# A two-layer decoder trunk in fp32: the depthwise convolution divided anew between TensorE and VectorE, and weights kept split for the second half

## The chip, the cores and the metric

The kernel runs on one core of one Trainium2 chip, in one launch. Its time is that of the device, in microseconds (us), from one execution to the next; the median of several runs is given. The engines named below are TensorE (PE: matrix products, with its weight loads PEld), VectorE (DVE), ScalarE (ACT), GpSimd (POOL) and SyncE (SP, which here issues the DMAs).

## The reference

The input x is 2048 rows of 1024 float32 numbers. Two layers with residuals follow, and a last RMSNorm. Layer 0 projects, pools over four windows, runs a state space scan, gates and projects back. Layer 1 is the one the change touches:

```
def _odd_mixer(h, w_in, conv_w, conv_b, ln_g, ln_b, w_out):
    proj = jnp.einsum('bsd,de->bse', h, w_in)
    val, gt, z = ...
    g = (val * jax.nn.sigmoid(gt)).astype(jnp.float32)
    c = lax.conv_general_dilated(
        g, kern, window_strides=(1,), padding=[(CONV_KERNEL - 1, 0)],
        dimension_numbers=('NWC', 'WIO', 'NWC'), feature_group_count=CONV_CHANNELS)
    c = c + conv_b.astype(jnp.float32)
    mu = jnp.mean(c, axis=-1, keepdims=True)
    cc = c - mu
    var = jnp.mean(cc * cc, axis=-1, keepdims=True)
    c = cc * lax.rsqrt(var + LN_EPS) * ln_g.astype(jnp.float32) + ln_b.astype(jnp.float32)
    y = (jax.nn.silu(c) * jax.nn.silu(z.astype(jnp.float32))).astype(h.dtype)
    return jnp.einsum('bse,ed->bsd', y, w_out)
```

The convolution is causal, 31 taps wide, one filter for each of the 1024 channels. The weight matrix w_in is 1024 x 3072.

## The kernel before

**Tiling.** The 2048 rows go in two halves of 1024, h = 0 ("A") and h = 1 ("B"). Activations lie with channels on the 128 partitions, so 1024 channels are eight channel tiles j = 0..7, and a tile of a half is 128 x 1024. A half has two blocks b of 512 rows. Layer 1 of the second half needs the last 30 columns of the first half's g.

**Products.** Each projection is done in fp32r with both sides split: a weight tile (128 x 1024, 512 KB) is loaded as `raw`, ScalarE casts it to `w` hi (L351), VectorE subtracts to get `w` lo (L319), and three products hi x hi, hi x lo, lo x hi are accumulated. A projection of one tile over a half is 48 matmuls of 512 columns, so a pair g, v of one j is 96. The thread `fetch_thread` loads, `split_thread` splits; `raw` has two slots and `w` eight. Each half loads and splits every weight again.

**Order.** A scheduler in Python fixes the program order of every engine before it is built: threads yield operations and waits, have a rank (`RANK`), take slots from pools (`act`, `w`, `st`, `ca`, `cg`, ...), and the planner's own cost for each operation decides who is next. The projections run in this order on TensorE: layer 0 of A, of B, out projection of A; layer 1 of A (pairs g, v for j in `ORDER[0]`, then y0..y7, the third projection z); out projection of B (B.glu, B.o); layer 1 of B (pairs in `ORDER[1]`, then y); the last projection of A (A.q) and of B (B.q).

**The convolution.** `post_val` makes g = v x sigmoid of the gate and stores it to `gd`. On VectorE, `conv_load` loads a tile with its 30 columns of halo as `cg`, ScalarE makes the first product with the bias into `ca`, and `conv_thread` adds 30 taps, each a SCALAR_TENSOR_TENSOR at L337 `ca <- cg, cwt, ca` that reads the sum which the one before it wrote. The last two tiles are done in two pieces of 512 columns. The result is stored to `cd`. Tiles in `PEC` are convolved on TensorE instead, in `pe_conv`: band matrices built by ScalarE are the weights (`act`), the tile comes from `gpd` with 64 columns a half, and four batches of 12 fp32 products are done for a tile (each product is two passes, so 24 instructions in the trace). Tiles in `PEB` are done this way for both halves in one go, at 128 columns; the rest of `PEC` for the second half alone, at 64. So before, tiles 6 and 7 are on TensorE in both halves, 4 and 5 in the second; VectorE has six tiles of the first half and four of the second.

**LayerNorm.** `ln_thread(h, b)` loads a block of all eight tiles from `cd` into four slots, adds them up on VectorE, and lets TensorE sum over partitions: a mean (`aux <- onesN, st`, 512 columns), the variances (four products of one column) and the broadcast of the scale (`aux <- ones, st`, four of 128 columns). In the trace each of these is a few rows of L401. `ln_out` multiplies with the gate and splits; A's two blocks go to `y1d`, from where `y1_thread` loads them for A.q.

## Time and profile before

| | |
|---|---|
| median of 3 runs | 1502.55 us (1501.55 to 1502.56) |
| the profiled execution, its own time | 1500.32 us |
| its span in the trace | 1498.5 us |
| mean granted TensorE clock | 0.995 |
| HBM read, written | 181.56 MB, 93.51 MB |

The profile lists, beside the busy time of each engine, the costliest groups of instructions. Two of them belong to the change: the taps, and the weight splits with the subtractions of layer 0's weights among them.

```profile
L337 DVE SCALAR_TENSOR_TENSOR ca<-cg,cwt,ca 128x1024 f32<-128x1024 f32 (+1 forms) x360 | 397.5, 1106 | 12.8 <-ACT ca L363 2.5
L319 DVE TENSOR_TENSOR w<-raw,w 128x1024 fp32r<-128x1024 f32 (+1 forms) x119 | 141.9, 1195 | 106.8 <-ACT w L351 106.1
L351 ACT CAST w<-raw 128x1024 fp32r<-128x1024 f32 (+1 forms) x119 | 121.6, 1022 | 214.9 <-PE mm L401 141.6
L401 PE MATMUL aux<-st,act 128*128 128x128 f32 (+2 forms) x448 | 63.8, 289 | 0.0
```

A row gives line, engine, operation, tiles, shapes and count, then busy time and the mean of one in ns, then the idle time of the engine ahead of them and what ended it. The 360 taps are 12 groups of 30: eight whole tiles and four pieces. The last row holds the convolution's batches and other small products.

### The profile page before, as it was taken

To read this page: it belongs to the slowest core of one execution; us is meant where nothing else is said; L and a number is where in the kernel's file an instruction comes from. 1 tells how busy PE (TensorE), PEld (TensorE's weight loads), DVE (VectorE), ACT (ScalarE), POOL (GpSimd) and SP (SyncE) were. 2 spreads that over 40 slices of the span, in tenths; PEclk is the share of its full clock that TensorE was granted. 3 is DMA by queue.
4 is the path that set the end of the run, shared out by engine and by line. 5 is a ranking of instruction groups with operands and counts; after the bars stand their busy time and mean duration, and the time that the engine had idled before them with its cause. 6 is when DMAs were issued, how large, how long until landed. Compare 5 with 4: busy or idle time off the path is not lost. (4 is left out here: it accounts for less than half of the span.)

```text
span 1498.5 us, 17919 instructions
## 1 busy us (share of the span) xinstructions
PE 1467.7 (98%) x6768; PEld 1202.1 (80%) x6768; DVE 1104.4 (74%) x1333; ACT 524.7 (35%) x834; POOL 89.7 (6%) x297
## 2 busy tenths in 40 slices
PE   7999899999999999999999999999999999999997
PEld 5887688888888888888888888888888788887785
DVE  7988583997975224699999998247987998987632
ACT  6235341112143035211111521352364556544411
POOL 1000100000000011000000000110000000003321
PEclk9999999999999999999999999999999999999999
DMA  9579946556475462331343543524557475957752
GB/s 350 197 212 335 336 165 247 194 189 239 161 268 151 125 206 85 112 111 59 99 127 113 210 140 128 183 70 128 109 156 227 138 244 185 385 202 248 260 171 109
DMA packets 161159, 276.26 MB, mean 184 GB/s; under 512 B 53184, under 2 KB 83632, under 8 KB 161072
## 3 DMA queue, kind: packets, MB, share of 16 engines
q1 hardware_dynamic: 161072, 275.12, 55.5%
q8 instruction: 53, 0.87, 0.2%
q14 instruction: 34, 0.28, 0.1%
HBM read 181.56 MB, written 93.51 MB: 184 GB/s over the span
## 5 line engine op out<-in xcount | busy, mean ns | idle before, releaser
L401 PE MATMUL mm<-act,w 128*128 128x512 f32 x4224 | 1003.8, 397 | 9.6 <-ACT act L363 6.6
L401 PEld LDWEIGHTS mm<-act,w 128*128 128x128 f32 x4224 | 793.2, 189 | 190.5 <-ACT act L363 6.6
L337 DVE SCALAR_TENSOR_TENSOR ca<-cg,cwt,ca 128x1024 f32<-128x1024 f32 (+1 forms) x360 | 397.5, 1106 | 12.8 <-ACT ca L363 2.5
L401 PE MATMUL mm<-w,act 128*128 128x512 f32 x1344 | 315.9, 395 | 0.8 <-DVE w L319 0.8
L401 PEld LDWEIGHTS mm<-w,act 128*128 128x128 f32 x1344 | 251.7, 188 | 59.4 <-DVE w L319 1.1
L319 DVE TENSOR_TENSOR w<-raw,w 128x1024 fp32r<-128x1024 f32 (+1 forms) x119 | 141.9, 1195 | 106.8 <-ACT w L351 106.1
L351 ACT CAST w<-raw 128x1024 fp32r<-128x1024 f32 (+1 forms) x119 | 121.6, 1022 | 214.9 <-PE mm L401 141.6
L363 ACT ACTIVATE junk<-st 128x1024 bf16<-128x1024 f32 (+1 forms) x64 | 54.0, 844 | 123.8 <-DVE st L319 116.1
L319 DVE TENSOR_TENSOR st<-st,mm 128x512 f32<-128x512 f32 x48 | 30.9, 683 | 76.2 <-PE mm L401 76.2
L351 ACT CAST act<-st 128x512 fp32r<-128x512 f32 (+1 forms) x64 | 51.8, 855 | 57.2 <-DVE st L337 16.6
L363 ACT ACTIVATE po<-mm 128x1024 f32<-128x1024 f32 x28 | 28.7, 1025 | 112.4 <-PE mm L401 70.7
L319 DVE TENSOR_TENSOR act<-st,act 128x512 fp32r<-128x512 f32 (+1 forms) x64 | 56.4, 922 | 14.7 <-ACT act L351 14.6
L401 PE MATMUL aux<-st,act 128*128 128x128 f32 (+2 forms) x448 | 63.8, 289 | 0.0
L363 ACT ACTIVATE act<-act,mask 128x128 f32<-128x128 f32 x192 | 58.0, 392 | 16.5 <-DMA act<-band 16.5
L401 PEld LDWEIGHTS aux<-st,act 128*128 128x128 f32 x448 | 57.2, 191 | 2.9
L363 ACT ACTIVATE st<-mm 128x1024 f32<-128x1024 f32 x24 | 24.6, 1024 | 81.5 <-PE mm L401 81.5
L337 DVE SCALAR_TENSOR_TENSOR act<-aux,vcol,act 128x512 fp32r<-128x512 f32 x32 | 22.6, 746 | 41.0 <-ACT act L363 41.0
L317 POOL TENSOR_TENSOR sml<-sml,mhalf 128x1 f32<-128x1 f32 (+2 forms) x38 | 30.3, 798 | 336.8 <-DVE sml L327 335.2
L351 ACT COPY st<-aux 128x256 f32<-128x256 f32 (+3 forms) x50 | 21.4, 445 | 75.2 <-PE aux L401 56.9
L329 POOL TENSOR_SCALAR sml<-sml 128x1 f32<-128x1 f32 (+2 forms) x72 | 25.7, 357 | 365.3 <-ACT junk L363 360.6
L401 PE MATMUL mm<-act,act 128*128 128x512 f32 x192 | 45.0, 394 | 0.8 <-DVE st L319 0.8
L337 DVE SCALAR_TENSOR_TENSOR st<-st,mm 128x1024 f32<-128x1024 f32 x24 | 34.2, 1424 | 14.7 <-PE mm L401 8.8
(144 smaller groups left out, 873.0 us busy)
## 6 DMA issues: line engine op xcount, KB each, us to landing
raw<-in_odd_w_in SPq DMA_DIRECT2D x48, 512.0 KB, 3.9
st<-x1d SPq DMA_DIRECT2D x48, 256.0 KB, 4.9
raw<-in_even_w_in SPq DMA_DIRECT2D x23, 512.0 KB, 5.7
st<-in_xT SPq DMA_DIRECT2D x16, 512.0 KB, 5.9
st<-in_x SPq DMA_DIRECT2D x16, 512.0 KB, 7.9
raw<-in_even_w_out SPq DMA_DIRECT2D x16, 512.0 KB, 3.9
z1d<-po SPq DMA_DIRECT2D x16, 512.0 KB, 3.2
st<-z1d SPq DMA_DIRECT2D x16, 512.0 KB, 6.5
```

Source lines behind the costliest of these rows:

```text
L317: return Op("G", d, [a, b], [o], lambda: G.tensor_tensor(o, a, b, op))
L319: return Op("V", d, [a, b], [o], lambda: V.tensor_tensor(o, a, b, op))
L329: e.tensor_scalar(o, a, s1, s2, op0, op1)
L337: return Op("V", d, rd, [o], lambda: V.scalar_tensor_tensor(o, a, s, b, op0, op1))
L351: return Op("A", adur(o, a, 0), [a], [o], lambda: A.copy(o, a))
L363: return Op("A", adur(o, a, n), rd, wr, lambda: A.activation(o, a, fn, **kw))
L401: nc.tensor.matmul(o, w, x, start=s, stop=e)
```

## The change

Five things change together.

- **Division.** `PEB` is empty and `PEC` is (5, 6, 7): TensorE convolves three tiles, of the second half alone. VectorE has all eight tiles of the first half and five of the second (0 to 4, of which 3 and 4 in pieces). `ORDER[1]` is (0, 1, 2, 6, 3, 7, 4, 5).
- **Two running sums.** A tile on VectorE has two sums, `ca` and `cb`. ScalarE makes the first product of each; taps 2 to 30 alternate between them (29 instructions), and one addition joins them. The pool `ca` has 4 slots instead of 2.
- **Kept weights.** The 24 weight tiles of layer 1's projections (wt for g, wv for v, w1z for z) are split once, for the first half; `keep_thread` stores hi and lo to DRAM (2 x 512 KB), and the second half loads both into `w` with no cast and no subtraction.
- **LayerNorm.** A's two blocks and B's second take their four slots from `ca`, B's first from `act`; B's blocks wait until A's second is done.
- **Planner and setup.** The planner's cost of an fp32 column is higher, and `dynamic_dma_scratch_size=1024` is given to the builder.

The core of the diff:

```diff
 SLOTS = dict(act=25, w=8, raw=2, st=8, po=2)
 NSSM = 3
-RANK = dict(split=2, pool=4, pec=3, lna=8, lnb=3, y1=3, ssm=4, prep=2)
-PEB = (6, 7)
-PEC = (4, 5) + PEB
-ORDER = (range(NK), (0, 1, 6, 7, 2, 3, 4, 5))
+KEEP = (("wt", "0", "1"), ("wv", "0", "1"), ("w1z", "0", "1"),)
+RANK = dict(keep=5, split=2, pool=4, pec=3, lna=8, lnb=3, y1=3, ssm=4, prep=2)
+PEB = ()
+PEC = (5, 6, 7)
+ORDER = (range(NK), (0, 1, 2, 6, 3, 7, 4, 5))

...
     slots("po", SLOTS["po"], SLOT)
     slots("cg", 2, SLOT)
-    slots("ca", 2)
+    slots("ca", 4)
     slots("sml", 12, 16)
...
                 d += width(o) / 2216.0
             elif w.shape[1] > 64:
-                d += max(0.224, width(o) * 1e-3)
+                d += max(0.224, width(o) * 1.68e-3)
             else:
...
             self.src, self.name, self.pool, self.key = src, name, "w", key

+            self.kept = self.like = None
+            self.refs = 1
+
         def release(self):
-            free(self.pool, self.hi, self.lo)
+            self.refs -= 1
+            if self.refs == 0:
+                free(self.pool, self.hi, self.lo)

...
     jobs_parts = {}

+    def keep(pairs):
+
+        for n, (a, b) in enumerate(pairs):
+            a.kept = [dram(f"kept{len(keeps)}_{p}", (128, 1024)) for p in "hl"]
+            a.refs = 2
+            b.like = a
+            keeps.append(a)
+
+    keeps = []
+
+    def keep_thread(job):
+        for d, t in zip(job.kept, (job.hi, job.lo)):
+            yield dma(d, t.bitcast(F32))
+        job.release()
+        done("kept", job)
+
     def fetch_thread(jobs):
+        prev = None
         for job in jobs:
+            if job.like:
+                if prev and not prev.like:
+                    yield Wait(("w", prev))
+                prev = job
+                yield Wait(("kept", job.like))
+                job.hi, job.lo = yield Alloc(job.pool, 2, F32R)
+                for d, t in zip(job.like.kept, (job.hi, job.lo)):
+                    yield dma(t.bitcast(F32), d)
+                done("w", job)
+                continue
+            prev = job
             job.raw = yield Alloc("raw")
...
     def split_thread(jobs):
         for job in jobs:
+            if job.like:
+                continue
             job.hi, job.lo = yield Alloc(job.pool, 2, F32R)
...
             free("raw", job.raw)
             done("w", job)
+            if job.kept:
+                spawn(keep_thread(job), RANK["keep"], "keep")

...
             cgt[h, j] = gt
             yield Wait(("cw",))
-            ca = cas[h, j] = yield Alloc("ca")
+            ca, cb = cas[h, j] = yield Alloc("ca", 2)
             yield act(ca[:, :H], gt[:, 0:H], AF.Identity, bias=vc("conv_b", j), scale=cwt[:, j, 0:1])
+            yield act(cb[:, :H], gt[:, 1:H + 1], AF.Copy, scale=cwt[:, j, 1:2])
             done("cg", h, j)
...
         for h, j, bl in seq:
             yield Wait(("cg", h, j))
-            gt, ca = cgt[h, j], cas[h, j]
+            gt, (ca, cb) = cgt[h, j], cas[h, j]
             n0, n1 = bl[0] * 512, bl[-1] * 512 + 512
-            acc = ca[:, n0:n1]
-            for k in range(1, NT):
-                yield stt(acc, gt[:, k + n0:k + n1], cwt[:, j, k:k + 1], acc, ALU.mult, ALU.add)
+            acc = ca[:, n0:n1], cb[:, n0:n1]
+            for k in range(2, NT):
+                yield stt(acc[k % 2], gt[:, k + n0:k + n1], cwt[:, j, k:k + 1], acc[k % 2], ALU.mult, ALU.add)
+            yield tt(acc[0], acc[0], acc[1], ALU.add)
             if bl[-1] == 1:
                 free("cg", gt)
+                free("ca", cb)
             spawn(conv_store(h, j, ca, bl), 6, f"cs{h}{j}")
...
         for j in range(NK):
             yield Wait(("c", h, j, b))
-        if h == 0 or b == 0:
-            ct = yield Alloc("act", 4)
-            pools = ("act",) * 4
-        else:
-            pools = ("ca", "ca", "cg", "cg")
-            ct = yield Alloc("ca", 2)
-            ct += yield Alloc("cg", 2)
+        pool = "act" if h == 1 and b == 0 else "ca"
+        pools = (pool,) * 4
+        ct = yield Alloc(pool, 4)
         cc = [c[:, :1024] for c in ct]
...
     out_units(1, "B.q", io["odd_w_out"], y1[1], evac1(1), True)

+    named = {j.name: j for j in jobs}
+    pairs = []
+    for j in jobs:
+        for pre, a, b in KEEP:
+            if j.name.startswith(pre + a):
+                pairs.append((j, named[pre + b + j.name[len(pre + a):]]))
+    keep(pairs)
+
     def main():
...
     spawn(y1_thread(0, y1[0], ("u", GATE_Y)), RANK["y1"], "y1A0")
     spawn(after((y1[0].name, 7, 0), y1_thread(1, y1[0], ("u", GATE_Y))), RANK["y1"], "y1A1")
-    spawn(ln_thread(1, 0, y1[1]), RANK["lnb"], "lnB0")
-    spawn(ln_thread(1, 1, y1[1]), RANK["lnb"], "lnB1")
+    spawn(ln_thread(1, 0, y1[1], (y1[0].name, NK - 1, 1)), RANK["lnb"], "lnB0")
+    spawn(ln_thread(1, 1, y1[1], (y1[0].name, NK - 1, 1)), RANK["lnb"], "lnB1")
     spawn(fnb_thread(0, ("u", "A.q.e0t3")), 4, "fnb")
...
     from concourse.bass_utils import run_bass_kernel_spmd

-    nc = bacc.Bacc("TRN2", target_bir_lowering=False, num_devices=1)
+    nc = bacc.Bacc("TRN2", target_bir_lowering=False, num_devices=1, dynamic_dma_scratch_size=1024)
     arrays, io = {}, {}
     for name, a in laid_out(inputs).items():
         a = np.ascontiguousarray(a)
```

What follows of this for the engines' program order is seen at three places.

TensorE, in layer 1 of the second half: the end of a projection's matmuls (`mm <- act, w`) and the start of a batch of the convolution (`aux <- st, act`). Before:

```order
L401 MATMUL mm_905_7732<-act_831_7118,w_885_7528 128x512
L401 MATMUL mm_905_7732<-act_865_7331,w_885_7528 128x512
L401 MATMUL aux_914_7825<-st_899_7681,act_901_7683 128x128
L401 MATMUL aux_914_7825<-st_899_7681,act_902_7684 128x128
L401 MATMUL aux_914_7825<-st_899_7681,act_903_7685 128x128
```

and with the change:

```order
L402 MATMUL mm_934_8174<-act_818_7171,w_916_7950 128x512
L402 MATMUL mm_934_8174<-act_855_7420,w_916_7950 128x512
L402 MATMUL aux_937_8188<-st_921_8040,act_923_8042 128x64
L402 MATMUL aux_937_8188<-st_921_8040,act_924_8043 128x64
L402 MATMUL aux_937_8188<-st_921_8040,act_925_8044 128x64
```

The columns of a product of this batch go from 128 (both halves) to 64 (one half); over the whole program 16 such batches become 12, and 48 products fall away.

VectorE, in layer 1 of the first half, where a tile's taps end and the next tile's begin; `w` with `raw` is a weight split, `st` with `mm` an evacuation. Before:

```order
L337 SCALAR_TENSOR_TENSOR st_612_4958<-st_612_4958,mm_611_4957 128x1024
L319 TENSOR_TENSOR w_618_5023<-raw_608_4907,w_617_5022 128x1024
L337 SCALAR_TENSOR_TENSOR ca_599_4822<-cg_598_4806,cwt,ca_599_4822 128x1024 x8
L319 TENSOR_TENSOR w_623_5088<-raw_615_4978,w_622_5087 128x1024
L337 SCALAR_TENSOR_TENSOR ca_599_4822<-cg_598_4806,cwt,ca_599_4822 128x1024 x3
L337 SCALAR_TENSOR_TENSOR ca_610_4927<-cg_609_4909,cwt,ca_610_4927 128x1024 x3
L337 SCALAR_TENSOR_TENSOR st_621_5086<-st_621_5086,mm_620_5085 128x1024
```

and with the change:

```order
L338 SCALAR_TENSOR_TENSOR ca_599_4876<-cg_597_4857,cwt,ca_599_4876 128x1024
L320 TENSOR_TENSOR w_624_5153<-raw_616_5044,w_623_5152 128x1024
L338 SCALAR_TENSOR_TENSOR ca_598_4875<-cg_597_4857,cwt,ca_598_4875 128x1024
L320 TENSOR_TENSOR ca_598_4875<-ca_598_4875,ca_599_4876 128x1024
L338 SCALAR_TENSOR_TENSOR ca_610_4991<-cg_609_4966,cwt,ca_610_4991 128x1024
L338 SCALAR_TENSOR_TENSOR ca_611_4992<-cg_609_4966,cwt,ca_611_4992 128x1024
L338 SCALAR_TENSOR_TENSOR ca_610_4991<-cg_609_4966,cwt,ca_610_4991 128x1024
L338 SCALAR_TENSOR_TENSOR ca_611_4992<-cg_609_4966,cwt,ca_611_4992 128x1024
```

Taps that followed one another on one sum now alternate between two, and an addition closes the tile.

VectorE, at the transition from the out projection of B to layer 1 of B: the last evacuation of B.o (`st` with `mm`), then the norm's pairs that make the second half's activations (`act <- aux, vcol, act`). Before:

```order
L319 TENSOR_TENSOR st_820_7062<-st_820_7062,mm_818_7060 128x512
L319 TENSOR_TENSOR w_840_7190<-raw_837_7153,w_839_7189 128x1024
L319 TENSOR_TENSOR w_846_7218<-raw_841_7191,w_845_7217 128x1024
L337 SCALAR_TENSOR_TENSOR act_853_7263<-aux_854_7264,vcol,act_852_7262 128x512
L337 SCALAR_TENSOR_TENSOR act_853_7263<-aux_855_7275,vcol,act_852_7262 128x512
L337 SCALAR_TENSOR_TENSOR act_857_7281<-aux_858_7291,vcol,act_856_7280 128x512
L337 SCALAR_TENSOR_TENSOR act_857_7281<-aux_859_7300,vcol,act_856_7280 128x512
```

and with the change, from the second instruction of the first pair on:

```order
L338 SCALAR_TENSOR_TENSOR act_856_7421<-aux_858_7434,vcol,act_855_7420 128x512
L338 SCALAR_TENSOR_TENSOR ca_785_6782<-cg_784_6771,cwt,ca_785_6782 128x1024
L338 SCALAR_TENSOR_TENSOR act_860_7441<-aux_861_7451,vcol,act_859_7440 128x512
L338 SCALAR_TENSOR_TENSOR act_860_7441<-aux_862_7460,vcol,act_859_7440 128x512
L338 SCALAR_TENSOR_TENSOR ca_786_6783<-cg_784_6771,cwt,ca_786_6783 128x1024
L338 SCALAR_TENSOR_TENSOR act_864_7467<-aux_866_7474,vcol,act_863_7466 128x512
L338 SCALAR_TENSOR_TENSOR act_864_7467<-aux_867_7487,vcol,act_863_7466 128x512
L338 SCALAR_TENSOR_TENSOR ca_785_6782<-cg_784_6771,cwt,ca_785_6782 128x1024
L338 SCALAR_TENSOR_TENSOR act_869_7494<-aux_870_7500,vcol,act_868_7493 128x512
L338 SCALAR_TENSOR_TENSOR act_869_7494<-aux_871_7513,vcol,act_868_7493 128x512
L320 TENSOR_TENSOR ca_785_6782<-ca_785_6782,ca_786_6783 128x1024
L320 TENSOR_TENSOR st_876_7560<-ca_872_7540,ca_873_7541 128x1024
```

The two weight splits between the evacuation and the first pair are gone, and seven taps of the first half's tile 7 (`ca <- cg, cwt, ca`) stand there; one more tap stands in each gap between the pairs, as the rows show, and the addition behind the last; the LayerNorm sums of A's first block (`st <- ca, ca`) follow right behind. On TensorE, 75 projection matmuls of layer 1 of B stand between the transposes of the last pair and this LayerNorm's first product, 48 between that product and its second one, and 18 between the second and the third. Behind the third, 816 projection matmuls and the twelve batches come before the first product of A's second block. In the program before, A's first LayerNorm stands in the midst of the second half's pairs.

## The prediction

> **What bounds the kernel now.** I read first the page's busy times, then the busy time by stage, then TensorE's own instructions in order of time, then VectorE's.
>
> ```profile
> span 1498.5 us, 17919 instructions
> PE 1467.7 (98%) x6768; PEld 1202.1 (80%) x6768; DVE 1104.4 (74%) x1333; ACT 524.7 (35%) x834; POOL 89.7 (6%) x297
> ```
>
> TensorE is busy for 1467.7 of 1498.5 us. By stage:
>
> ```profile
> 560.00:900.00 340.00, 339.83 (x1502) 277.08 (x1502) 295.12 (x255) 95.17 (x112) 7.89 (x32) 1.00 0.37 116
> 900.00:1010.00 110.00, 109.83 (x510) 90.14 (x509) 53.37 (x54) 36.83 (x50) 12.77 (x48) 1.00 0.38 130
> 1010.00:1310.00 300.00, 299.13 (x1505) 250.42 (x1504) 262.81 (x271) 148.79 (x294) 5.46 (x10) 1.00 0.64 196
> 1310.00:1500.00 190.00, 176.73 (x773) 142.21 (x771) 107.90 (x118) 63.57 (x110) 43.60 (x122) 0.98 0.57 196
> ```
>
> A row of a stage gives its bounds, its length, then busy time of TensorE (PE), its weight loads, VectorE (DVE), ScalarE (ACT) and GpSimd. TensorE is idle for 0.17 us of the 340 us of layer 1's first half, for 0.17 and 0.87 us in the next two stages, and the clock is whole. So TensorE's queue is the bound: what leaves it shortens the run one for one, and what makes it wait lengthens it. VectorE has 45 us free in the first of these stages (340 - 295), 57 in the second (110 - 53), 37 in the third (300 - 263).
>
> ```profile
> 1075.35 2.84 PE L401 MATMUL aux<-st,act 128*128 128x128 f32 x24
> 1077.94 1.64 PE L401 MATMUL mm<-act,w 128*128 128x512 f32 x6
> ...
> 1191.02 2.79 PE L401 MATMUL aux<-st,act 128*128 128x64 f32 x24
> 1193.62 4.42 PE L401 MATMUL mm<-act,w 128*128 128x512 f32 x18
> ...
> 1270.46 32.23 PE L401 MATMUL mm<-act,w 128*128 128x512 f32 x138
> 1302.53 7.83 PE L401 MATMUL mm<-w,act 128*128 128x512 f32 x33
> ```
>
> Columns: start, length, what. A batch of the convolution on TensorE (12 products, 24 instructions) takes 1077.94 - 1075.35 = 2.59 us at 128 columns and 2.60 us at 64. A projection's matmul takes 32.07/138 = 0.232 us here; the first stage's 1502 in 339.83 us give 0.226, and I use 0.229.
>
> **TensorE: the term.** Before, four channel tiles run on TensorE, two of them for both halves at once; four batches each, 16 x 2.6 = 41.6 us. Now three tiles run there, second half only: 12 x 2.6 = 31.2. **That removes 10.4 us.** The other matmuls are the same in number.
>
> Here a rule speaks for more. The Trainium skill, "TensorE: Matmul & The Clock Gate", section "Step-by-step: what each phase is for", has throughput as purely one column per cycle; by it a 64-column batch would cost 1.3 us, before 31.1 and now 15.6, so 15.5 us less and some 5 us more gain. The two rows above disagree (2.59 and 2.60), and I go by them.
>
> **VectorE: three tiles more, each cheaper.**
>
> ```profile
> 692.31 1.22 DVE L319 TENSOR_TENSOR w<-raw,w 128x1024 fp32r<-128x1024 f32 x1
> 693.45 10.53 DVE L337 SCALAR_TENSOR_TENSOR ca<-cg,cwt,ca 128x1024 f32<-128x1024 f32 x8
> ...
> 848.59 1.28 DVE L337 SCALAR_TENSOR_TENSOR ca<-cg,cwt,ca 128x1024 f32<-128x1024 f32 x1
> 849.79 1.22 DVE L319 TENSOR_TENSOR w<-raw,w 128x1024 fp32r<-128x1024 f32 x1
> ...
> 855.36 1.29 DVE L319 TENSOR_TENSOR act<-st,act 128x512 fp32r<-128x512 f32 x2
> 856.57 1.28 DVE L337 SCALAR_TENSOR_TENSOR ca<-cg,cwt,ca 128x1024 f32<-128x1024 f32 x1
> 857.77 0.68 DVE L319 TENSOR_TENSOR act<-st,act 128x512 fp32r<-128x512 f32 x1
> ...
> 1165.13 0.74 DVE L337 SCALAR_TENSOR_TENSOR ca<-cg,cwt,ca 128x512 f32<-128x512 f32 x1
> 1165.79 2.06 DVE L337 SCALAR_TENSOR_TENSOR st<-st,mm 128x1024 f32<-128x1024 f32 x1
> ...
> 1220.48 14.93 DVE L337 SCALAR_TENSOR_TENSOR ca<-cg,cwt,ca 128x512 f32<-128x512 f32 x19
> ```
>
> Eight taps that each need the one before take 10.53: 1.316 a step. A tap whose next instruction is another's lasts 1.28, but that next one starts after 1.20 (856.57 to 857.77); and the tap at 856.57 itself starts 0.08 before its neighbour ends (855.36 + 1.29), its own running sum last touched earlier. With two sums every tap is in that place: 1.20. At 512 columns it is 14.93/19 = 0.786 chained and 0.66 not. A split or sum lasts 1.22 and the next starts 1.14 later.
>
> A tile then costs 29 x 1.20 + 1.14 = 35.9 us instead of 30 x 1.316 = 39.5 (the first product of the second sum goes to ACT). Before: six tiles of the first half, two whole and two in pieces (60 x 0.786 = 47.2): 8 x 39.5 + 2 x 47.2 = 410. Now eight and three whole and two in pieces (58 x 0.66 + 1.2 = 39.5): 11 x 35.9 + 2 x 39.5 = 474. So 64 more; the 24 weight splits that vanish from the second half return 24 x 1.14 = 27. VectorE gets **37 us more**, 1141 of the span: below TensorE, so no bound by its sum. The question is the order.
>
> **Does VectorE keep pace?** Between two evacuations of the first half, TensorE does 96 matmuls, 22.0 us; VectorE now 15 taps (18.0), two splits (2.28), one evacuation (1.14) and every second time a sum: 21.4 or 22.6. VectorE is full there but keeps pace. The two extra tiles run on through 900 to 1003, where it had 57 us free. In the second half, from LayerNorm of the first block on, it is full again.
>
> **What that fullness costs at three places.** First the transition, where the last row tiles become the second half's activations:
>
> ```profile
> 982.91 1.29 DVE L319 TENSOR_TENSOR st<-st,mm 128x512 f32<-128x512 f32 x2 [1.99 <-PE mm L401]
> 984.12 1.22 DVE L319 TENSOR_TENSOR w<-raw,w 128x1024 fp32r<-128x1024 f32 x1
> ...
> 992.09 1.41 DVE L337 SCALAR_TENSOR_TENSOR act<-aux,vcol,act 128x512 fp32r<-128x512 f32 x2 [3.92 <-ACT act L363]
> 995.06 1.41 DVE L337 SCALAR_TENSOR_TENSOR act<-aux,vcol,act 128x512 fp32r<-128x512 f32 x2 [1.57 <-ACT act L363]
> ...
> 1000.99 1.41 DVE L337 SCALAR_TENSOR_TENSOR act<-aux,vcol,act 128x512 fp32r<-128x512 f32 x2 [1.55 <-ACT act L363]
> ```
>
> TensorE's next row, and the landings of the convolution's stores and loads:
>
> ```profile
> 1000.43 29.80 PE L401 MATMUL mm<-act,w 128*128 128x512 f32 x128
> DMA to landing us min/median/max: 2.6/5.6/8.6
> ```
>
> The changed order puts seven taps (8.4) where the two splits stood, 984.12 to 992.5, 0.4 past the first pair's old start, and one tap (1.2) into each gap of 1.55. The last tap and the sum of tile 7 then end near 1003.5. From there the tile must be stored, loaded as LayerNorm's operand (the last row: cd's DMAs land after 2.6, 5.6 or 8.6) and summed (1.14 + 0.6): 1003.5 + 11.2 + 1.7 = 1016.4, between 1010 and 1022. TensorE comes to the first LayerNorm product after 75 projection matmuls behind the transposes, 1000.43 + 75 x 0.229 = 1017.6. At median landings that is 1.2 in time, at late ones 4.8 too late. Wait: **1.0** (0 to 5), nearer the median. In the old order that LayerNorm came 150 us later.
>
> Second, its third reduction now stands 18 instead of 24 matmuls behind the second:
>
> ```profile
> 1165.35 1.10 PE L401 MATMUL aux<-st,onesN 128*128 128x512 f32 x2 [0.45 <-DVE st L319]
> ...
> 1178.00 1.05 PE L401 MATMUL aux<-onesN,st 128*128 128x1 f32 x8 [0.42 <-DVE st L319]
> 1178.91 5.81 PE L401 MATMUL mm<-act,w 128*128 128x512 f32 x24
> 1184.56 1.05 PE L401 MATMUL aux<-st,ones 128*128 128x128 f32 x8
> ```
>
> With 24 nothing waited. VectorE has four 128-column scalings and POOL's small work in between; 6 x 0.229 = 1.4 less cover gives a wait of **1.0** (0 to 1.4). The old two waits, 0.45 + 0.42 = 0.9, go with the old order.
>
> Third, the LayerNorm of the first half's second block now follows all of the second half's taps.
>
> ```profile
> L337 DVE SCALAR_TENSOR_TENSOR st<-st,mm 128x1024 f32<-128x1024 f32 x24 | 34.2, 1424 | 14.7 <-PE mm L401 8.8
> ```
>
> From that third reduction TensorE has 816 matmuls and the 12 batches before it: 816 x 0.229 + 31.2 = 218.1. VectorE has three whole tiles (107.7), two in pieces (79.0), eight LayerNorm sums (9.1), four small scalings (put at 0.4 each, below a 512-column tap), six evacuations (6 x 1.424 = 8.5), then store, load and sum (11.2 + 1.7): 218.8. That is 0.7 late at median landings, nothing at early ones and 7 at late ones; the mean over such a spread is what I take. Wait: **2.0** (0 to 7).
>
> **Loads and the other engines.** ScalarE loses 24 weight casts and gains 16 first products (13 tiles x 2 instead of 10); it is 35% busy, and both lie beside TensorE's work. The stores of the first half's split weights are 48 x 0.5 MB and the second half loads 24 MB in place of 12.
>
> ```profile
> raw<-in_odd_w_in SPq DMA_DIRECT2D x48, 512.0 KB, 3.9
> q1 hardware_dynamic: 161072, 275.12, 55.5%
> ...
> 972.64 1.03 PE L415 MATMUL aux<-ident,st 128*128 128x128 f32 x8
> ```
>
> 36 MB on 275 take the queue from 55.5% to some 63%. A kept load waits in SP's queue until TensorE has freed two weight slots; behind it stand stores of gd and x1d and loads of cg, so a late slot delays the taps too. First place: slots come free by 972.64, a load takes 3.9, two in a row 7.8, so 980.4 against 982.71 of need. I put **0.5** (0 to 5) there and nothing in the steady part, where a pair's weights have 22 us. The smaller DMA scratch I cost at nothing: all but 87 packets run on the hardware queue; the trace shows no price for it, so I bound it by one median landing either way, -5.6 to 5.6, and take nothing, as the row of the queue says.
>
> Sum: -10.4 + 1.0 + 1.0 - 0.9 + 2.0 + 0.5 = -6.8. The profiled execution took 1500.32, span 1498.5; the median of the runs is 2.2 above, 1502.55. So 1493.5 by the one, **1495.5** as a median (-7.0, rounded).
>
> **The rivals.** *Nothing waits.* The landings fall early, the slack of the first half (340 - 295 before, some 10 after) covers all: -10.4 - 0.9, with some tenths of the stages' other waits: 1489.5 to 1493. For it: TensorE's waits in the stages above are below 0.9 each now. Against: the chain to LayerNorm begins at 1003.5 whatever happens.
>
> *The late operands decide.* The bounds above all high, or SP's queue standing on a kept load: 5 + 1.4 + 7 + 5 - 0.9 = 17.5 at most; six tenths of that, with -10.4, is no change: 1499.5 to 1505.5.
>
> *Two sums gain nothing (slower).* If a tap takes 1.316 with either sum, the first half has 232 steps (8 x 29) x 0.116 = 27 us more on VectorE against 10 of slack, so 17 of stall, and the second half (87 whole, 116 in pieces) 87 x 0.116 + 116 x 0.126 = 25 on a stretch without slack: 42 - 7 = 35 slower, 1537. The whole is even where the stretch loses 7 of stall, from about 1.24 us a tap. For it: nearly all taps of the trace stand in chains at 1.316. Against: 856.57 to 857.77 and 1165.13 to 1165.79, where the same instruction without a dependent next one took 1.20 and 0.66. The Trainium skill, "VectorE: DVE Perf Modes", section "The DRAIN you can't avoid", says that a next operation doesn't start until the pipe is empty, and that this can't be skipped by chaining without semaphores; by that rule alternation would bring nothing, and the time would be that of this rival. The rows just named, with 0.08 of overlap, disagree.
>
> *The batches were hidden.* If TensorE had idled beside them, removing four would bring nothing, and the added waits would be left: 3.6 slower, 1506. The stage that holds them shows 0.87 us of idle time in 300; 2% at most.
>
> **How the numbers follow.** Forecast (1493 to 1499.5): 54%. Nothing waits (1489.5 to 1493): 18%. Late operands (1499.5 to 1505.5): 17%. Slower: two sums that gain nothing, with what queues up behind them, 9%, hidden batches 2%. A measurement of this kernel tells 0.2%, 3 us, from no change: faster, below 1499.5, is 0.54 + 0.18 = 0.72; within 0.2% it is 0.17, slower 0.09 + 0.02 = 0.11. The range from 1490 to 1502 takes the forecast, most of the best case and about half of the late one.
>
> **What would show it.** Right: taps in the changed profile start every 1.20 us (0.66 in pieces); 12 batches of 2.6; TensorE's idle time between 560 and 1310 no more than 5 us above before's 1.2; LayerNorm's first product near 1018 with 1 us before it, and its next one with about 2. Wrong: taps at 1.3; a projection matmul whose wait is released by a DMA of w (late kept weights); a stage of the first half with TensorE waiting for VectorE's evacuations; fewer than 10 us gone from TensorE's busy time of 1467.7.

## The result

The changed kernel takes 1528.57 us (median of 4 runs, 1525.23 to 1529.97), the kernel before 1502.55: a ratio of 1.0167, 95% interval 1.0144 to 1.0189. It is **slower by 26 us**; 7 us faster were forecast, and the range ended at 1502. The profiled execution took 1525.23 us, 24.9 more than that of before (1500.32).

The head of its page, and its stages (bounds, length, busy time of TensorE, its weight loads, VectorE, ScalarE and GpSimd, then granted clock, DMA share and GB/s):

```profile
span 1523.5 us, 17840 instructions
PE 1468.1 (96%) x6672; PEld 1195.9 (79%) x6672; DVE 1155.0 (76%) x1399; ACT 496.2 (33%) x772; POOL 108.1 (7%) x296
```

```profile
250.00:560.00 310.00, 307.62 (x1338) 250.59 (x1337) 197.25 (x314) 77.43 (x108) 6.08 (x30) 1.00 0.60 198
560.00:900.00 340.00, 339.73 (x1505) 276.77 (x1504) 293.85 (x264) 106.90 (x123) 8.86 (x37) 1.00 0.55 191
900.00:1010.00 110.00, 99.36 (x441) 80.83 (x440) 96.42 (x89) 29.48 (x39) 32.20 (x49) 0.96 0.46 158
1010.00:1310.00 300.00, 299.12 (x1467) 249.30 (x1466) 262.39 (x285) 112.19 (x228) 3.63 (x10) 1.00 0.58 192
1310.00:1520.00 210.00, 189.49 (x806) 151.15 (x805) 118.04 (x125) 70.13 (x116) 44.98 (x122) 0.96 0.62 210
```

Three things stand out. TensorE has 96 instructions fewer (6768 to 6672), and yet its busy time did not fall: 1468.1 after 1467.7. It idles for 10.6 of the 110 us from 900 to 1010, where it had idled for 0.17. And in that same stage GpSimd is busy for 32.20 us with 49 instructions, where 48 took 12.77.

The place is the transition to the second half's layer 1, the one at which the prediction put seven taps. TensorE's rows there, then VectorE's, then GpSimd's chain of small operations (the norm's 1/sqrt for two row tiles), from timelines of the changed kernel; columns are start, length, what, and in brackets the idle time ahead with what ended it.

```profile
1001.76 0.38 PE L416 MATMUL aux<-ident,st 128*128 128x128 f32 x2
1008.38 0.47 PE L416 MATMUL aux<-ident,st 128*128 128x128 f32 x1 [6.24 <-ACT st L364]
1009.42 1.33 PE L416 MATMUL aux<-ident,st 128*128 128x128 f32 x5 [0.56 <-ACT st L364]
1010.40 3.09 PE L402 MATMUL mm<-act,w 128*128 128x512 f32 x9
1013.33 1.03 PE L416 MATMUL aux<-ident,st 128*128 128x128 f32 x8
1014.12 2.32 PE L402 MATMUL mm<-act,w 128*128 128x512 f32 x9
```

```profile
996.93 1.28 DVE L320 TENSOR_TENSOR st<-st,mm 128x512 f32<-128x512 f32 x2
998.13 8.46 DVE L338 SCALAR_TENSOR_TENSOR ca<-cg,cwt,ca 128x1024 f32<-128x1024 f32 x7
1010.65 1.61 DVE L338 SCALAR_TENSOR_TENSOR act<-aux,vcol,act 128x512 fp32r<-128x512 f32 x2 [4.07 <-ACT act L364]
```

```profile
998.88 0.57 POOL L330 TENSOR_SCALAR sml<-sml 128x1 f32<-128x1 f32 x1 [8.72 <-ACT junk L364]
999.54 1.46 POOL L318 TENSOR_TENSOR sml<-sml,mhalf 128x1 f32<-128x1 f32 x1
1001.08 0.77 POOL L318 TENSOR_TENSOR sml<-sml 128x1 f32<-128x1 f32 x1
1001.93 1.11 POOL L318 TENSOR_TENSOR sml<-sml,sml 128x1 f32<-128x1 f32 x1
1003.13 2.31 POOL L330 TENSOR_SCALAR sml<-sml 128x1 f32<-128x1 f32 x2
1005.40 1.59 POOL L318 TENSOR_TENSOR sml<-sml,mhalf 128x1 f32<-128x1 f32 x1
1006.96 0.19 POOL L318 TENSOR_TENSOR sml<-sml,sml 128x1 f32<-128x1 f32 x1
...
1007.92 0.19 POOL L318 TENSOR_TENSOR sml<-sml,sml 128x1 f32<-128x1 f32 x1
```

Before, the same chain ran from 984.87 to 989.69, with rows such as these:

```profile
985.47 0.54 POOL L317 TENSOR_TENSOR sml<-sml,mhalf 128x1 f32<-128x1 f32 x1
986.09 0.19 POOL L317 TENSOR_TENSOR sml<-sml 128x1 f32<-128x1 f32 x1
...
987.05 1.52 POOL L317 TENSOR_TENSOR sml<-sml,mhalf 128x1 f32<-128x1 f32 x1
```

On one column per partition a GpSimd operation takes 0.19 or 0.54 us while VectorE is idle (also behind 1006.9, when the taps are over), and 0.57 to 1.59, mostly about a whole tap (1.28), while taps run back to back. The chain takes 9.2 us instead of 4.8. ScalarE's scaling waits for the chain, the transposes wait for ScalarE (6.24 + 0.56), and when TensorE starts again its clock is halved: nine matmuls take 3.09 us at 1010.40, and 2.32 at 1014.12, where the clock is whole again. The norm of the block before, 33 us earlier, shows the same: seven taps run from 963.53 to 971.99, the chain takes 8.1 us where it took 3.5 in the kernel before, and the transposes wait 3.12 + 0.71 us. The stretch of the second norm in a window row:

```profile
1004.00:1012.00 8.00, 3.06 (x10) 2.48 (x11) 3.83 (x5) 3.57 (x4) 3.78 (x8) 0.58 0.01 2
1422.00:1432.00 10.00, 5.19 (x12) 4.15 (x13) 7.11 (x6) 2.27 (x4) 2.13 (x7) 0.50 0.64 219
```

The second row is a stall of the last stage. Of the three longest waits there, the last one, 6.12 us, is for a weight split:

```profile
1340.68 1.13 PE L402 MATMUL aux<-st,onesN 128*128 128x512 f32 x2 [2.59 <-DVE st L320]
1385.15 1.05 PE L402 MATMUL aux<-onesN,st 128*128 128x1 f32 x8 [2.76 <-DVE st L320]
1426.81 3.78 PE L402 MATMUL mm<-w,act 128*128 128x512 f32 x8 [6.12 <-DVE w L320]
```

**The account of the 24.9 us.** TensorE's waits of 0.15 us and more add up to 45.5 us, before to 21.7: 23.8 more. By place: the two sets of transposes at the transition 10.6 (before 0.2), LayerNorm's products 7.0 (2.0), weights in the last stage 7.4 (0.8), layer 0's scan between 290 and 410 2.3 (0); the start gives 0.6 back. TensorE's busy time is up by 0.4 (and 0.6 more of the span stands behind its last matmul) although 10.4 us of batches left it, so about 10.8 came in elsewhere. The clock accounts for most of it: TensorE is busy for 26.2 us in stretches at half speed, before for 6.8, and half of the difference, 9.7, is an estimate of what this cost. Of that, 3.0 lies at the transition, 4.3 in the last stage, and 2.4 in the first 200 us, where TensorE waited no longer than before. The changed order of layer 0's scan adds some 1.5 of busy time (worked out below, at the kernel before with the new cost). The stretches of the transition and of the last stage:

```profile
974.52:977.93 3.41, 2.96 (x10) 2.58 (x11) 1.62 (x3) 1.77 (x3) 0.00 (x0) 0.50 0.02 5
1005.24:1012.06 6.82, 3.12 (x10) 2.54 (x11) 2.65 (x4) 3.57 (x4) 2.62 (x7) 0.50 0.01 2
1387.53:1390.94 3.41, 3.41 (x9) 2.64 (x8) 1.82 (x2) 0.83 (x3) 2.86 (x8) 0.50 0.90 299
1421.66:1431.90 10.24, 5.09 (x12) 4.07 (x13) 7.11 (x6) 2.50 (x4) 2.47 (x8) 0.50 0.62 211
```

### The profile page after: what moved, and what is told of

It is laid out like the page before. It is cut to its first block, busy times and chain, and to the rows that moved or that the text cites. A ratio compares the mean times of both kernels' runs of the same rounds, so it can differ in the third digit from the quotient of the medians.

```text
span 1523.5 us, 17840 instructions
## 1 busy us (share of the span) xinstructions
PE 1468.1 (96%) x6672; PEld 1195.9 (79%) x6672; DVE 1155.0 (76%) x1399; ACT 496.2 (33%) x772; POOL 108.1 (7%) x296
## 3 DMA queue, kind: packets, MB, share of 16 engines
q1 hardware_dynamic: 147920, 308.92, 59.5%
## 5 line engine op out<-in xcount | busy, mean ns | idle before, releaser
L402 PE MATMUL mm<-act,w 128*128 128x512 f32 x4224 | 1005.1, 397 | 10.4 <-ACT act L364 7.2
L338 DVE SCALAR_TENSOR_TENSOR ca<-cg,cwt,ca 128x1024 f32<-128x1024 f32 (+1 forms) x435 | 463.4, 1136 | 4.0 <-ACT ca L364 4.0
L402 PE MATMUL mm<-w,act 128*128 128x512 f32 x1344 | 320.8, 399 | 7.4 <-DVE w L320 6.4
L402 PEld LDWEIGHTS mm<-w,act 128*128 128x128 f32 x1344 | 255.3, 191 | 67.0 <-DVE w L320 7.1
L320 DVE TENSOR_TENSOR w<-raw,w 128x1024 fp32r<-128x1024 f32 (+1 forms) x95 | 112.3, 1186 | 80.9 <-ACT w L352 73.8
L352 ACT CAST w<-raw 128x1024 fp32r<-128x1024 f32 (+1 forms) x95 | 96.6, 1018 | 135.2 <-PE mm L402 98.2
L320 DVE TENSOR_TENSOR act<-st,act 128x512 fp32r<-128x512 f32 (+1 forms) x64 | 56.5, 921 | 24.9 <-ACT act L352 24.6
L318 POOL TENSOR_TENSOR sml<-sml,mhalf 128x1 f32<-128x1 f32 (+2 forms) x38 | 34.4, 905 | 352.1 <-DVE sml L328 350.4
L402 PE MATMUL aux<-st,act 128*128 128x64 f32 (+1 forms) x352 | 53.0, 293 | 1.4 <-DVE st L320 1.2
L330 POOL TENSOR_SCALAR sml<-sml 128x1 f32<-128x1 f32 (+2 forms) x72 | 33.7, 467 | 271.3 <-ACT junk L364 266.5
L402 PEld LDWEIGHTS aux<-st,act 128*128 128x128 f32 x352 | 45.6, 191 | 6.0 <-DVE st L320 3.5
L364 ACT ACTIVATE act<-act,mask 128x128 f32<-128x128 f32 x144 | 43.3, 391 | 8.7 <-DMA act<-band 8.7
```

Source lines behind the costliest of these rows:

```text
L318: return Op("G", d, [a, b], [o], lambda: G.tensor_tensor(o, a, b, op))
L320: return Op("V", d, [a, b], [o], lambda: V.tensor_tensor(o, a, b, op))
L330: e.tensor_scalar(o, a, s1, s2, op0, op1)
L338: return Op("V", d, rd, [o], lambda: V.scalar_tensor_tensor(o, a, s, b, op0, op1))
L352: return Op("A", adur(o, a, 0), [a], [o], lambda: A.copy(o, a))
L364: return Op("A", adur(o, a, n), rd, wr, lambda: A.activation(o, a, fn, **kw))
```

## The experiments

Each kernel is the changed one with the edit shown, unless another base is named. The kernel before ran beside each group, at 1503 to 1504 us.

**Taps held back at the norms.**

```diff
             for k in range(2, NT):
+                for e in range(2):
+                    if h == 0 and ("x1t", 1, 4 * e + 3) in sc.keys:
+                        yield Wait((h1[1].name, 0, e))
...
         ct = yield Alloc(pool, 4)
+        done("ln", h, b)
...
+            if h == 1:
+                yield Wait(("ln", 0, 0))
             ca, cb = cas[h, j] = yield Alloc("ca", 2)
```

> The changed kernel, with the taps of the first half's last tile held back in VectorE's order: none between the last evacuation of a block's out projection and the first pair of that block's norm. LayerNorm of A's first block keeps its place ahead of the second half's taps. Theory A (the taps that run back to back slow GpSimd's small operations of the norm, 9.2 us where they took 4.8; TensorE then stands, and its clock is halved for some us): GpSimd's chain of the last pair is back at 4.6 to 5.5 us, TensorE's idle time at the two sets of transposes falls from 10.6 to at most 2, the two half-speed stretches there go; the taps held come later, so up to 8 us are lost again at the first product of A's second LayerNorm. Total 1513 to 1523. Rival B (the norm is late for another reason, such as an evacuation or ScalarE): the chain stays near 9 us and the total at 1526 to 1532.

Measured: 1519.49 us. GpSimd's chain took 3.9 us, the transposes' waits fell from 10.6 to 1.6, and the clock stayed whole there:

```profile
993.88 0.54 POOL L318 TENSOR_TENSOR sml<-sml,mhalf 128x1 f32<-128x1 f32 x1
994.50 0.19 POOL L318 TENSOR_TENSOR sml<-sml 128x1 f32<-128x1 f32 x1
...
997.40 0.33 PE L416 MATMUL aux<-ident,st 128*128 128x128 f32 x1 [0.89 <-ACT st L364]
998.44 0.77 PE L416 MATMUL aux<-ident,st 128*128 128x128 f32 x5 [0.71 <-ACT st L364]
998.96 2.32 PE L402 MATMUL mm<-act,w 128*128 128x512 f32 x9
```

Nothing else on the norm's path was touched, so theory A holds here. Some of the gain was lost again, though not at A's second LayerNorm itself (0.88 us of wait, as without the hold) but behind it: the last projection waited 8.04 us at 1328 for the activations that this LayerNorm makes. So the taps held back were not free later either.

**No gate on B's LayerNorms.**

```diff
-    spawn(ln_thread(1, 0, y1[1], (y1[0].name, NK - 1, 1)), RANK["lnb"], "lnB0")
-    spawn(ln_thread(1, 1, y1[1], (y1[0].name, NK - 1, 1)), RANK["lnb"], "lnB1")
+    spawn(ln_thread(1, 0, y1[1]), RANK["lnb"], "lnB0")
+    spawn(ln_thread(1, 1, y1[1]), RANK["lnb"], "lnB1")
```

> The changed kernel without the new gate on the two LayerNorms of B. Theory C (the gate pushes B's LayerNorms into the last stage, where weight splits queue behind them): the idle time of 9.6 us at 1385 and 1427 and the half-speed stretches behind it go, 8 to 12 us less, 1517 to 1521. Rival D (the last stage is late because A's second LayerNorm comes late, whatever the gate): within 3 us of 1528.6.

Measured: 1521.05 us (1517.18 to 1525.15), 7.5 less than the changed kernel, just short of what theory C asked; the spread of 8 us leaves the size uncertain. The waits for weights fell from 7.4 to 4.0, but one of 3.29 us for LayerNorm at 1383 stayed. The gate is a part of the loss, not all of it.

**The planner's old cost.**

```diff
-                d += max(0.224, width(o) * 1.68e-3)
+                d += max(0.224, width(o) * 1e-3)
```

> The changed kernel with the planner's old cost of an fp32 column. Theory E (the new cost reorders layer 0, whose 2.3 us of waits at 296 to 409 were not there before): those waits go, 2 to 4 us less, 1525 to 1527. Rival: the waits stay, and the time within 1.5 us of 1528.6.

Measured: 1510.66 us, 17.9 less, where theory E had 2 to 4. The scan's waits are gone, as theory E said, but so are the waits for weights in the last stage. Between the two profiled executions 14.6 us lie: 9.9 of waits and 4.0 of TensorE's busy time (1464.1). Of the edits made to the changed kernel alone, this one gained most. It undoes a number that only the planner reads, and I had not costed it.

**Taps held, and no gate.** The edits of the first two runs together, and nothing else.

> Taps held as in the first of these runs, and no gate on B's LayerNorms. If theories A and C hold and the two places do not touch each other, the gains add up: 1502 to 1513. If the taps held only move the wait to A's second LayerNorm, no better than the better one of the two alone.

Measured: 1536.81 us, slower than either and than the changed kernel. The second branch ("no better than the better one") allows for that, but it did not foresee a loss. A's second LayerNorm and the next one now overlap (first products at 1293.72 and 1303.27), and one wait for the last projection's activations took 20 us:

```profile
1334.23 2.05 PE L402 MATMUL aux<-st,ones 128*128 128x128 f32 x8 [9.59 <-DVE st L328]
1356.38 5.87 PE L402 MATMUL mm<-w,act 128*128 128x512 f32 x16 [20.09 <-ACT act L352]
```

**Old cost, and taps held at the second norm only.** The edit of the third run, and that of the first with one line changed:

```diff
-                for e in range(2):
+                for e in (1,):
```

> The changed kernel with the planner's old cost, and the taps held back as in the first run, but only ahead of the norm of the second block. Theory A: against 1510.7 of the run with the old cost alone, the 6.8 us of idle time at the second set of transposes and the half-speed stretch behind it go, 6 to 9 us less: 1502 to 1505. If the held taps make A's second LayerNorm and with it the last projection late, as in the first run, half or all of that is lost: 1505 to 1511.

Measured: 1511.8 us, no gain over 1510.66. The waits at the second set of transposes fell from 6.8 to 1.6; the last stage lost as much, with waits of 0.3 to 2.4 us for activations, weights and LayerNorm between 1326 and 1416 and ten us of halved clock at their end. That is the second branch of the expectation, 0.8 past its far end.

**The kernel before with the new cost.**

```diff
-                d += max(0.224, width(o) * 1e-3)
+                d += max(0.224, width(o) * 1.68e-3)
```

> The kernel before with the planner's new cost of an fp32 column alone; TensorE's order then differs only in layer 0's scan. Theory E: 2 to 4 us slower than before, with waits of 0.3 to 0.7 us between 290 and 410 that before does not have. Rival: within 1.5 us of before.

Measured: 1507.78 us, a ratio of 1.0029 (1.0016 to 1.0042): 4.5 slower. Five waits of 0.29 to 0.73 us stand between 297 and 410, which is 2.2 together; a wait for LayerNorm at 1172 is 1.25 instead of 0.45. TensorE's order differs between 265 and 425 alone, in layer 0's scan. From the wait near 169 to the norm's transposes near 585, TensorE needs 420.8 us here, less an estimated 1.7 for a stretch of halved clock at 170, and 415.3 before: 3.8 more, of which waits are 2.4 (with small ones) and TensorE's busy time the rest. That and LayerNorm's 0.8 about make up the 4.5.

**Old cost, no kept weights.**

```diff
-KEEP = (("wt", "0", "1"), ("wv", "0", "1"), ("w1z", "0", "1"),)
+KEEP = ()
```

> The changed kernel with the planner's old cost, and with no kept weights: the second half casts and splits its weights again. Theory F (VectorE has no room in the second half, so the 27 us of splits show up as late LayerNorms): 6 to 25 us slower than 1510.7. Rival G (36 MB of stores and loads cost more than the splits): 1505 to 1510.

Measured: 1532.76 us, 22.1 more than 1510.66. The 36 MB cost less than the splits: with the splits back, VectorE is busy 1184.1 us instead of 1155.8, and the last projection waits 15.85 us for A's activations at 1348.

**Old cost, one running sum.**

```diff
-            acc = ca[:, n0:n1], cb[:, n0:n1]
-            for k in range(2, NT):
-                yield stt(acc[k % 2], gt[:, k + n0:k + n1], cwt[:, j, k:k + 1], acc[k % 2], ALU.mult, ALU.add)
-            yield tt(acc[0], acc[0], acc[1], ALU.add)
+            acc = ca[:, n0:n1]
+            for k in range(1, NT):
+                yield stt(acc, gt[:, k + n0:k + n1], cwt[:, j, k:k + 1], acc, ALU.mult, ALU.add)
...
-            yield act(cb[:, :H], gt[:, 1:H + 1], AF.Copy, scale=cwt[:, j, 1:2])
```

> The changed kernel with the planner's old cost and one running sum for a tile, 30 chained taps. Theory H (two sums save 0.116 us a tap; 13 tiles cost 47 us more on VectorE without them, of which the first half and the stage from 900 to 1010 hide some 25): 15 to 45 us slower than 1510.7. Rival (two sums gain nothing on a full VectorE): within 3 us of 1510.7, with taps that start every 1.20 to 1.24 us either way.

Measured: 1555.39 us, 44.7 more. The taps take 512.7 us where they took 463.4 in the changed kernel, or 479.6 with the 15 additions that join the two sums. The last projection waits 17.41 and 15.52 us for the activations of A's first and second block. In this run, too, GpSimd's chain was slow beside the taps (9.3 us): whether there is one sum or two makes no difference to that.

**Tile 7 on TensorE in both halves.** The batches of both halves cost what those of one do (2.6 us), so a tile in `PEB` that is in `PEC` anyway takes 36 us off VectorE for nothing.

```diff
-PEB = ()
+PEB = (7,)
-ORDER = (range(NK), (0, 1, 2, 6, 3, 7, 4, 5))
+ORDER = (range(NK), (0, 1, 7, 2, 6, 3, 4, 5))
-                d += max(0.224, width(o) * 1.68e-3)
+                d += max(0.224, width(o) * 1e-3)
...
-        pool = "act" if h == 1 and b == 0 else "ca"
-        pools = (pool,) * 4
-        ct = yield Alloc(pool, 4)
+        if h == 0 or b == 0:
+            ct = yield Alloc("act", 4)
+            pools = ("act",) * 4
+        else:
+            pools = ("ca", "ca", "cg", "cg")
+            ct = yield Alloc("ca", 2)
+            ct += yield Alloc("cg", 2)
...
-    spawn(ln_thread(1, 0, y1[1], (y1[0].name, NK - 1, 1)), RANK["lnb"], "lnB0")
-    spawn(ln_thread(1, 1, y1[1], (y1[0].name, NK - 1, 1)), RANK["lnb"], "lnB1")
+    spawn(ln_thread(1, 0, y1[1]), RANK["lnb"], "lnB0")
+    spawn(ln_thread(1, 1, y1[1]), RANK["lnb"], "lnB1")
```

> The changed kernel with the planner's old cost, tile 7 on TensorE in both halves at once (PEB = (7,), so its four batches have 128 columns and there are still 12 batches), the second half in the order 0, 1, 7, 2, 6, 3, 4, 5, and LayerNorm's slots and gates as before the change. Kept weights and two sums stay. Theory A: VectorE has no taps left at the norms of the second half, so the waits of 10.6 us there and the halved clock are gone, and the 10.4 us of the four batches are seen: 1491 to 1497. If the loss of the changed kernel lies in what stays (kept weights, two sums, 12 batches), it stays above 1503.

Measured: **1492.5 us**, a ratio of 0.9922 (0.9910 to 0.9935) to before: 10.75 us faster, faster than both kernels. Its page and stages:

```profile
PE 1456.7 (98%) x6672; PEld 1189.8 (80%) x6672; DVE 1121.2 (75%) x1369; ACT 495.9 (33%) x769; POOL 92.1 (6%) x296
...
900.00:1010.00 110.00, 109.29 (x507) 89.43 (x506) 66.87 (x67) 32.48 (x45) 15.26 (x48) 1.00 0.42 144
1010.00:1310.00 300.00, 300.00 (x1460) 249.55 (x1459) 272.54 (x293) 121.06 (x234) 5.35 (x10) 1.00 0.71 232
```

TensorE has the same 6672 instructions as the changed kernel and is busy for 11.4 us less; against before it is 11.0 less, with 10.4 forecast. The waits sum to 21.0 (before 21.7), GpSimd's 48 instructions are down to 15.26 us. The run undoes the gate, LayerNorm's slots and the planner's cost along with the division, so it does not share out the gain among them; what it shows is that 12 batches, two sums and kept weights are together worth the 10 us in an order without taps beside the norms.

**Tiles 6 and 7 in both halves.** Against the run before this one:

```diff
-PEB = (7,)
+PEB = (6, 7)
-ORDER = (range(NK), (0, 1, 7, 2, 6, 3, 4, 5))
+ORDER = (range(NK), (0, 1, 6, 7, 2, 3, 4, 5))
```

> The same with tiles 6 and 7 on TensorE in both halves (still 12 batches; VectorE has six tiles and five) and the second half in the old order 0, 1, 6, 7, 2, 3, 4, 5. Theory A: the transposes wait for nothing, 1490 to 1497, unless B's second LayerNorm, which stands late in TensorE's order here, is waited for: then 1497 to 1505.

Measured: 1495.5 us, ratio 0.9938 (0.9919 to 0.9957). The transposes wait 0.7 us; B's second LayerNorm is waited for, 4.18 us at 1385 with a halved clock behind it. VectorE is 36 us emptier (1085.3) and nothing is gained by it.

**Tile 7 in both halves, no kept weights.** Against the kernel of 1492.5 us:

```diff
-KEEP = (("wt", "0", "1"), ("wv", "0", "1"), ("w1z", "0", "1"),)
+KEEP = ()
```

> The kernel of 1492.5 us (tile 7 on TensorE in both halves) without kept weights: the second half splits its 24 weight tiles again. VectorE is busy for 272 of 300 us between 1010 and 1310 there. Theory F (the 27 us of splits have no room in the second half): LayerNorms come late, 4 to 15 us slower, 1496 to 1508. Rival G (the transfers cost more than the splits): 1487 to 1492.

Measured: 1495.37 us, ratio 0.9944 (0.9922 to 0.9966). The interval overlaps with that of the run with kept weights, so their worth here is at most some 8 us, where it was 22 us in the fuller kernel. Inconclusive between F and G.

**Tile 7 in both halves, new cost.** Against the kernel of 1492.5 us:

```diff
-                d += max(0.224, width(o) * 1e-3)
+                d += max(0.224, width(o) * 1.68e-3)
```

> The kernel of 1492.5 us with the planner's new cost of an fp32 column. If that cost does its harm in layer 0's scan alone, as it did in the kernel before (4.5 us slower with it): 1495 to 1499, with the three waits of 0.4 to 0.7 us between 290 and 410. If it also disorders the last stage, as the step from 1528.6 to 1510.7 us suggests: 1500 to 1512, with waits for weights behind 1330.

Measured: 1498.98 us, ratio 0.9974 (0.9954 to 0.9993): 6.5 more, with the scan's five waits (2.2 us) and no wait for weights behind 1330 above 0.8 us. The same part of layer 0 needs 420.8 us, again less 1.7 for the clock, where it takes 415.3 with the old cost. So the cost does steady harm there; the further harm in the last stage of the changed kernel came with that kernel's own order.

## Why the prediction was wrong

**The term on TensorE was right.** Four batches less give the 10.4 us that were forecast; a batch at 64 columns takes 2.59 us in the changed kernel as well (1120.40 to 1122.99), and the ninth run shows 11.0 us less of busy time. The Trainium skill's rule of one column per cycle, from the page and section named in the prediction, did not hold at this size.

```profile
1120.40 2.79 PE L402 MATMUL aux<-st,act 128*128 128x64 f32 x24
1122.99 1.65 PE L402 MATMUL mm<-act,w 128*128 128x512 f32 x6
```

**VectorE's prices for a step were right.** Seven taps take 8.46 us with two sums (1.20 a step), 29 half-width ones 19.31 (0.66), and TensorE idled for 0.27 of the 340 us of the first half. The rival on two sums fell with it, and with 44.7 us in the eighth run. The sum over the steps was too low: VectorE is busy for 50.6 us more, not 37, mainly as the taps of before take 397.5 us and not 410. Nor was VectorE full in the first half (293.85 of 340 us): it did the added taps in the next stage, where it is busy for 96.42 us instead of 53.37, beside the norms.

```profile
1223.80 19.31 DVE L338 SCALAR_TENSOR_TENSOR ca<-cg,cwt,ca 128x512 f32<-128x512 f32 x29
```

**The step that failed** is this one: "The changed order puts seven taps (8.4) where the two splits stood, 984.12 to 992.5, 0.4 past the first pair's old start". I checked VectorE's own queue, and on it the sum is right: the taps end in time. But the gap of 3.92 us ahead of that pair was the time in which GpSimd and ScalarE worked, and I took GpSimd's chain as fixed. The taps stretched it from 4.8 to 9.2 us, and that of the norm before, which the prediction did not look at, from 3.5 to 8.1. TensorE's waits for it, 10.6 us at the two norms, fall to 1.6 with the taps held; the prediction has none there. The trace of before could have warned: at 987.05 an operation of 0.54 us took 1.52, beside the weight split of 986.94 to 988.17. The Trainium skill, "GPSIMD Engine Reference", section "1. Specifications", says that GpSimd's way to the on-chip memory is shared with VectorE, with contention when an instruction there has two inputs from it. A tap has two, and the trace agrees, with 0.19 us against 0.57 to 1.12.

**The second thing left out** is the price of a stall beyond its length. The prediction counted waits one for one. The halved clock cost an estimated 9.7 us more than before, nearly what the four batches save, and 7.3 of it behind the waits of the transition and the last stage. The Trainium skill, "TensorE: Matmul & The Clock Gate", section "Part 1: The HAM clock gate (the "warmup" mystery)", tells of half rate after an idle window of about 3.4 us; the 6.24 us here agree, but in the changed kernel 2.76 us at 1385.15 were also followed by it (a mean clock of 0.57 from 1387 to 1391), and 2.59 us at 1340.68 were not.

**The four waits I did cost** came to nearly nothing: LayerNorm's first product at the transition (1.0 forecast) and its third reduction (1.0) waited for nothing, the first kept weights (0.5) neither, A's second LayerNorm 0.88 (2.0). Two other places were not looked at: the last stage, where B's LayerNorms, weight splits and the final norm's GpSimd chains meet, and layer 0, where the planner's cost moved the scan; the three places named in the section on the change leave out this fourth. The planner's cost stands in the change's list, but the prediction's sum has no term for it and gives no reason. With the old cost the changed kernel is 17.9 us faster, so this term is as much a failed step as the taps.

**The signs.** TensorE's idle time between 560 and 1310 came to 11.8 us, where at most 6.2 was to show that the forecast is right. "Fewer than 10 us gone from TensorE's busy time" was to show that it is wrong and came true, but it misleads: the batches did go, and the halved clock and the scan hid them.

**The rivals.** "The late operands decide" had the right kind of event, late operands, at other places, and its bound of 17.5 us of waits was passed (23.8). None of the rivals held the measured time, and the chance of 0.11 for a slower kernel was given to other mechanisms.

**What stays open.** The first and fifth runs show that the last stage gives back much of what is saved at the transition, and the fourth that two helpful edits can harm together; which order there would suit the division of the changed kernel was not found. Why the planner's cost does so much more harm in the changed kernel's last stage than elsewhere was not followed. The smaller DMA scratch stayed in every run; the ninth, which has it, gains what was forecast for the batches, so it left no loss to be seen. The slowing of GpSimd was shown by moving taps away, not by adding them to a kernel that had none; but the length of the chain follows what VectorE does beside it: 3.5 us with nothing (ninth run), 3.9 with one tap (first run), 4.8 with two weight splits (before), 9.2 with seven taps.

## What to carry to other kernels

An idle stretch of an engine is not free room when a small serial chain on another engine runs beside it: before filling VectorE's gap, ask what GpSimd does in it, and look for one of its rows that is longer beside a busy VectorE. Where TensorE is busy 98% of the time, price a stall of some us at about 1.3 of its length, since the clock is halved behind it: here 10.6 us of waits at the transition brought 3.0 more, and 13.5 in the last stage 4.3. And a constant of the planner is an edit like any other: follow it through every stage that it can reorder, not only the one it was meant for.

## What the runs showed of the hardware

Small GpSimd operations beside back-to-back VectorE taps take up to a tap and a quarter (1.28 us), 0.57 to 1.59 us instead of 0.19 to 0.54, with one chained sum as well as with two alternating ones. In the changed kernel TensorE's clock falls to half for 3.4, 6.8 or 10.2 us around a stall. It stayed there for 34 us in the fourth run, in which TensorE was busy for 5.63 of them. And in the twelfth it was halved at 1173 with no wait of 0.15 us or more near it, right behind LayerNorm's one-column products of 1172.22. The fourth run's row, then the twelfth's:

```profile
1326.00:1360.00 34.00, 5.63 (x16) 4.16 (x17) 25.97 (x26) 18.40 (x23) 4.21 (x4) 0.50 0.74 245
1173.00:1176.50 3.50, 3.50 (x11) 2.82 (x11) 3.16 (x6) 2.29 (x2) 2.66 (x4) 0.51 0.32 88
```

With the split weights stored and loaded, the traffic rose from 276 to 310 MB and the queue's share from 55.5% to 59.5%. No wait of TensorE in the changed kernel is put down to these transfers; on VectorE one weight split, at 620.74, waits 5.20 us for such a store.
